# One attention group in steps of two items, with the copy of values in 17 parts and a later norm and split in the filling

## The chip, the cores and the metric

The kernel runs on one core of a Trainium2 chip. Its time is the device time of one execution in microseconds; given are the median of the runs shown and, from one profiled execution, where the time went. The core has five engines with a queue each, which run side by side and wait for one another by semaphores: PE (matrix products and transposes), DVE and ACT (element work on rows, both can read PE's result banks), POOL (element work in on-chip memory) and SP (here: it starts transfers). ACT starts some transfers too. Each engine takes its instructions strictly in the order in which they were queued.

## The reference, cut to what matters

One layer of a bidirectional encoder on 2048 tokens of 1024 numbers, in float32:

```
u   = rmsnorm(x, g_pre_mix)
qa, ka, va, qb, kb, vb = split(u @ w_in)
o_a = rmsnorm(windowed_gqa_sink(qa, ka, va, table, sink_a), g_out_a)
o_b = rmsnorm(dilated_mixture(qb, kb, vb, table), g_out_b)
h   = x + rmsnorm(concat(o_a, o_b) @ w_o, g_post_mix)
h   = h + rmsnorm(relu(rmsnorm(h, g_pre_mlp) @ w_up)**2 @ w_down, g_post_mlp)
h   = h + rmsnorm(sigmoid(h @ w_g + b_g) * (p @ w_p), g_post_ple)
```

Group a (`windowed_gqa_sink`) has 8 heads of 64 numbers. A block of 128 queries sees the key block before it, its own and the next; the logits get a bias by relative position, and a sink logit per head joins maximum and denominator. Group b (`dilated_mixture`) has 8 heads and three patterns (dilation 1, 4, 16), whose outputs are mixed by a softmax over their log-denominators.

## The kernel before

Every float32 product of the projections and of the feed-forward part is made of three: each factor is split into a high part (rounded to the fast float32 format) and the low rest, and high x high, high x low and low x high are summed. In the attention, products are plain float32.

The stages in order: projection of the first tokens and of the values; group a; group b; output projection with the first norms; feed-forward part; gate and output. From group a on, the order on each engine is the order in which the program writes the instructions (`manual_schedule`).

*Group a.* An item is a pair of heads and a block of 128 queries; there are 4 x 16 = 64 items, numbered 0 to 63. `a_item` gives an item four stages:
- `scores` (L502): two products on PE, one for each head of the pair, into two of the three banks of `ps_s`. For the blocks in the middle a row has 384 keys, for the first and last block of a pair 256.
- `probs`: first `normalise` for the item before (L479 on DVE: reciprocal of the denominators; L481 on POOL: two scalings). Then a small copy on POOL (L509, the sink logit), and for each head on DVE bias and row minimum in one (L513) and on ACT the exponential with its row sum (L517). L513 is what frees a bank of scores.
- `turn` (L526): PE transposes the probabilities into the two banks of `ps_t`, DVE (L531) and ACT (L529) copy them out.
- `values` (L542): the products with the values into the one bank of `ps_o`; ACT copies four items out (L547).

`Pipe` runs them shifted against each other. At step t it issues the scores of item t, the values of item t-3, the transposes of item t-2, the probabilities of item t, and then calls `feed(t)`. `later(dt, fn)` files work under a later step, and `tick()` at the end of a step issues what is due.

*The pieces in group a.* `feed` takes one piece of a generator, `rest_of_qk`, that makes the projections of group b's q and k for the second half of the tokens: 8 chunks of weights, for each two halves of tokens, for each of these one sum over 8 parts in a bank of `psm`. `mm3_pieces` yields after each two parts, so a piece is six products of 512 columns (L173 to L175) and there are 64. After the last piece of a sum the generator goes on at the next call: ACT copies the bank out (L229, L231) and starts the store. Between pieces the next chunk's weights are loaded, scaled and split, two parts in a step: the high half on ACT (L132), the low half on DVE directly behind it (L133). Five pieces run ahead of the loop.

Transfers also lie in the loop: `prefetch_a` loads the next pair's q in halves and its bias, and POOL reorders them two steps later (L235, L458). Ahead of the loop `relay_v` copies group b's values in DRAM to another layout, in three transfers (L375, L377).

*Group b.* Items of 2 x 2 blocks, three patterns and 4 pairs of heads: 96 items. Pattern 16 sees one key block (128 columns), the others two (256). PE order in a step: scores (L752), values (L796), transposes (L779), then `feed_b`. This takes a piece of `wo_first` in three of four steps: the first half of the output projection, for group a's result, tile by tile of 128 tokens. A tile has four calls: norm and first piece; second piece and evacuation (L898); first piece of the second half, then the split of the next tile; second piece and evacuation. `norm` (L612) is a product with a column of ones into a bank of `ps_t`, followed by one operation on DVE and one on POOL. The split (`halves`) takes ACT (L128 high, L605 squares), DVE (L129 low) and POOL (L606, L607). The lines of `wo_first` that matter:

```
ro = norm()
...
if hf == 0 and n == 0:
    halves, norm = load_o(wop, raws, "wraw", ps_t, "pt", oad, t + 1)
if hf == 1 and n == 0:
    nxt = halves()
```

Of the kernel before, what the change touches and what calls it, by code (L numbers as in the profile page):

```python
# [59 lines left out]
def layer(ctx, tc, a, out):  # L60
# [43 lines left out]
    gains = {}  # L104
# [7 lines left out]
    def row_ap(v, off, ap):  # L112
        return bass.AP(tensor=v.tensor, offset=v.offset + off, ap=ap)
# [54 lines left out]

    load_gain("pre_mix", a["g_pre_mix"])

    def mm3_pieces(ps, n, lh, ll, rh, rl, per=2):
        for k in range(n):
            pe.matmul(ps, lh(k), rh(k), start=k == 0, stop=False)  # L173
            pe.matmul(ps, lh(k), rl(k), start=False, stop=False)  # L174
            pe.matmul(ps, ll(k), rh(k), start=False, stop=k == n - 1)  # L175
            if k % per == per - 1:
                yield

    def run(gen):
# [33 lines left out]
    def proj_chunk(w, c, tb, psm, pst, tag):  # L213
        uh, ul = u[tb]
        ps = psm.tile([128, 512], F32, name="psm", tag="psm")
        yield from mm3_pieces(ps, 8, lambda k: w[:, 0, k], lambda k: w[:, 1, k], lambda k: uh[:, k], lambda k: ul[:, k])
        t = sg.tile([128, 512], F32, name="sgt", tag="sgt")
        if c == VA0:
            evac(t, ps)
            pt = pst.tile([128, 4, 128], F32, name=tag, tag=tag)  # L220
            for j in range(4):
                pe.transpose(pt[:, j, :], t[:, 128 * j : 128 * j + 128], ident)
            t = sg.tile([128, 512], F32, name="sgt", tag="sgt")
            evac(t, pt.rearrange("p j n -> p (j n)"))
            act.dma_start(vad[512 * tb : 512 * tb + 512, :].rearrange("(j a) n -> a j n", j=4),
                         t.rearrange("a (j n) -> a j n", j=4))
            return
        if c < 512 or 768 <= c < 1280:
            act.activation(t, ps, AF.Copy, scale=-0.125)  # L229
        else:  # L230
            act.activation(t, ps, AF.Copy)  # L231
        act.dma_start(qkd[chunk_of[c]][:, 512 * tb : 512 * tb + 512], t)
# [112 lines left out]


    att_ps = ExitStack()
    psm = att_ps.enter_context(tc.tile_pool(name="psm", bufs=2, space=PSUM, reuse_waits="tile"))
    ps_o = att_ps.enter_context(tc.tile_pool(name="ps_o", bufs=1, space=PSUM, reuse_waits="tile"))
    ps_t = att_ps.enter_context(tc.tile_pool(name="ps_t", bufs=2, space=PSUM, reuse_waits="tile"))  # L350
    ps_s = att_ps.enter_context(tc.tile_pool(name="ps_s", bufs=3, space=PSUM, reuse_waits="tile"))
    ordered = att_ps.enter_context(ExitStack())
    ordered.enter_context(tc.manual_schedule(engines=set(ORDERED)))

    HH = [slice(0, 64), slice(64, 128)]
    attb = ExitStack()
# [15 lines left out]

    def relay_v():
        n = 8 * VROW
        sp.dma_start(row_ap(vb1o, 0, [[n, 16], [VCHUNK, 15], [1, n]]), row_ap(vb3, 4 * VROW, [[VCHUNK, 16], [n, 15], [1, n]]))  # L375
        for i, a0 in ((0, 0), (2, 112)):
            sp.dma_start(row_ap(vb1a, i * VCHUNK, [[n, 16], [VCHUNK, 2], [1, n]]),  # L377
                         row_ap(vb3, a0 * VROW, [[VCHUNK, 16], [n, 2], [1, n]]))

    def load_v(pair, p):  # L380
        c0 = 128 * pair
# [39 lines left out]
    class Pipe:  # L421
# [18 lines left out]
        def drain(self):  # L440
            for _ in range(3):
                self.step()

    st_b = {}
    with ExitStack() as st:
        ap2 = st.enter_context(tc.tile_pool(name="ap2", bufs=1, reuse_waits="tile"))
# [27 lines left out]
                later(2 * i, lambda start=start: later(2, start()))  # L474

        def normalise():
            e, dn, off = st_a["rd"].pop(0)
            rd = sml.tile([128, 2], F32, name="rd", tag="rd")
            dve.reciprocal(rd, dn)  # L479
            for hh in range(2):  # L480
                pool.tensor_scalar(e[:, hh, off:384], e[:, hh, off:384], rd[:, hh : hh + 1], 1.0,  # L481
                                   op0=ALU.mult, op1=ALU.mult)

        def a_item(pair, n):
# [18 lines left out]
                              kk.rearrange("p r (k a) -> p k r a", a=8), start=True, stop=True)  # L503

            def probs():
                if st_a["rd"]:
                    normalise()
                e = box["e"] = ep.tile([128, 2, 392], F32, name="e", tag="e")
                pool.tensor_copy(e[:, :, 384], nsink[:, 2 * pair : 2 * pair + 2])  # L509
                dn = sml.tile([128, 2], F32, name="dn", tag="dn")  # L510
                for hh in range(2):
                    tm = sml.tile([128, 1], F32, name="tm", tag="tm")
                    dve.tensor_tensor_reduce(  # L513
                        e[:, hh, off:384], box["ps"][hh][:, 0:w], box["b"][hh][:, boff : boff + w], scale=1.0,
                        scalar=nsink[:, 2 * pair + hh : 2 * pair + hh + 1], op0=ALU.add, op1=ALU.min, accum_out=tm,
                    )
                    act.activation(e[:, hh, off:385], e[:, hh, off:385], AF.Exp, bias=tm, scale=-1.0,  # L517
                                   accum_out=dn[:, hh : hh + 1])
                st_a["rd"].append((e, dn, off))
# [29 lines left out]
                if n == 15:  # L549
                    act.dma_start(oad[128 * pair : 128 * pair + 128], st_a["o"])  # L550

            return scores, probs, turn, values

        def rest_of_qk():
            cs = [c for p in range(4) for c in (768 + 128 * p, 1280 + 128 * p)]
            w = w_next
            for i, c in enumerate(cs):
                nxt = raw = None
                for n, tb in enumerate((2, 3)):
                    for m, _ in enumerate(proj_chunk(w, c, tb, psm, ps_t, "pt")):  # L560
                        if i < 7 and n == 0 and m == 0:
                            raw = load_raw(cs[i + 1])
                            nxt = wcp.tile([128, 2, 8, 128], F32R, name="wc", tag="wc")
                        if i < 7 and 4 * n + m >= 3:
                            j = 4 * n + m - 3
                            split_chunk(nxt, raw, range(2 * j, min(2 * j + 2, 8)))
                        yield
                w = nxt

        fill = rest_of_qk()  # L570
        for _ in range(5):
            next(fill)
        for kb in range(16):
            sp.dma_start(va[:, kb, :], row_ap(vad, 8 * kb * 128, [[128 * 128, 16], [128, 8], [1, 128]]))
        relay_v()

        def feed(t):
            if t == 57:
                st_b["q"] = load_q(0)
                st_b["k"] = {0: load_k(0)}  # L580
# [3 lines left out]
                st_b["text"] = [load_text(1, hh) for hh in range(2)]  # L584
            next(fill, None)

        pipe = Pipe(feed)
        pipe.push([a_item(pair, n) for pair in range(4) for n in range(16)])
        normalise()
        pipe.drain()  # L590
        run(fill)
    att_a.close()
    u23.close()

# [58 lines left out]
    with ExitStack() as st:  # L653
# [222 lines left out]
        def wo_first():  # L876
# [4 lines left out]
            oh_, ol_ = halves()  # L881
            yield
            for t in range(16):
                ro = norm()
                for hf in range(2):
                    cs = slice(512 * hf, 512 * hf + 512)
                    ps = psm.tile([128, 512], F32, name="psm", tag="psm")
                    for n, _ in enumerate(mm3_pieces(ps, 4, lambda k: oh_[:, k, :], lambda k: ol_[:, k, :],
                                                     lambda k: wa[k][0][:, cs], lambda k: wa[k][1][:, cs])):
                        if t < 15:  # L890
                            if hf == 0 and n == 0:
                                halves, norm = load_o(wop, raws, "wraw", ps_t, "pt", oad, t + 1)
                            if hf == 1 and n == 0:
                                nxt = halves()
                        if n == 0:
                            yield
                    mx = sg.tile([128, 512], F32, name="sgt", tag="sgt")
                    act.activation(mx, ps, AF.Copy, scale=ro)  # L898
                    act.dma_start(mad[128 * t : 128 * t + 128, cs], mx)
                    yield  # L900
                if t < 15:
                    oh_, ol_ = nxt

        def ple():
            pw = [pl.tile([128, S], F32R, name="pw", tag=tag).rearrange("p (k n) -> p k n", k=2)
# [703 lines left out]
```

## Time and profile before

| | |
|---|---|
| median of 3 runs | 2789.16 us (2787.52 to 2789.19) |
| profiled execution | 2785.3 us, its span 2783.5 us |
| PE busy | 2709.7 us (97%) |
| weight loads of PE | 2126.0 us (76%) |
| DVE busy | 1755.0 us (63%) |
| ACT busy | 1272.0 us (46%) |
| POOL busy | 932.5 us (33%) |

Matmuls overlap, and their ends are modelled: a matmul that is slow to be followed by the next still counts as busy until its modelled end, so short waits of PE show better in the starts of its instructions than in its busy time. The idle time of an engine that nothing waits for costs nothing.

### The profile page before, as it was taken

The page shows a single profiled execution, that of the slowest core. Times are in us where ns is not written, and L with a number is a line of the kernel's source. Part 1 is how long each engine was busy: PE and PEld are TensorE (multiplying, and loading weights), DVE is VectorE, ACT ScalarE, POOL GpSimd, SP SyncE. Part 2 cuts the span into 40 slices and gives each one's busy share as a digit, 9 for nine tenths or more (in the row PEclk, how much of TensorE's full clock was granted, in tenths as well). Part 3 has the DMA queues.
Part 4 walks back from the last instruction along what each step waited for, and adds up shares of the span by engine and source line. Part 5 has one row for each costly group of instructions (what it writes and reads, how often), then busy time and mean ns, then how long its engine had stood idle before and what let it go on. Part 6 is the DMA issues. An engine that isn't in the chain of part 4 may idle for free.

```text
span 2783.5 us, 38953 instructions
## 1 busy us (share of the span) xinstructions
PE 2709.7 (97%) x13952; PEld 2126.0 (76%) x13952; DVE 1755.0 (63%) x3423; ACT 1272.0 (46%) x2947; POOL 932.5 (33%) x950
## 2 busy tenths in 40 slices
PE   7999999998999999999999999999999999999998
PEld 6878866666676777787888888888888888887877
DVE  4210234446666563677777777777777778887675
ACT  4321345556555564556444444344544344443422
POOL 3000033341323211435344354354354354353230
PEclk9999999999999999999999999999999999999999
DMA  6232252315424324873222222225323223334463
GB/s 179 78 122 80 99 159 75 113 62 156 130 70 129 90 96 150 274 258 101 90 65 76 69 65 74 78 100 203 115 75 106 81 79 99 108 100 172 169 212 106
DMA packets 247874, 324.39 MB, mean 117 GB/s; under 512 B 19905, under 2 KB 175553, under 8 KB 245281
## 3 DMA queue, kind: packets, MB, share of 16 engines
q1 hardware_dynamic: 220544, 281.73, 32.1%
q10 hardware_dynamic: 27136, 40.18, 4.0%
q8 instruction: 110, 1.80, 0.3%
q14 instruction: 84, 0.68, 0.1%
HBM read 227.16 MB, written 102.04 MB: 118 GB/s over the span
## 4 chain that ended last, share of the span: by engine, by line
PE 53%; DVE 1%; DMA 0%; issue 0%; ACT 0%; POOL 0%; DVEq 0%; POOLq 0%; SPq 0%; ACTq 0%
PE psd L1294 13%; PE psy L1294 10%; PE psu L175 9%; PE psu L173 8%; PE psu L174 8%; PE psm L139 2%; PE psm L138 2%; PE psm L137 2%; PE pst L146 0%; DVE dnl L1133 0%; DMA h<-hd 0%; DVE y L1565 0%; DMA upraw<-in_w_up_dram 0%; DVE al L1133 0%; DVE upl L1157 0%
## 5 line engine op out<-in xcount | busy, mean ns | idle before, releaser
L1303 DVE TENSOR_TENSOR acc<-acc,psd 128x512 f32<-128x512 f32 x488 | 332.3, 685 | 189.2 <-PE psd L1294 183.6
L175 PE MATMUL psu<-vt,upl 128*128 128x512 f32 x1024 | 406.8, 397 | 0.0
L173 PE MATMUL psu<-vt,uph 128*128 128x512 f32 x1024 | 404.7, 395 | 0.0
L174 PE MATMUL psu<-vt,uph 128*128 128x512 f32 x1024 | 400.5, 391 | 0.0
L1138 POOL TENSOR_TENSOR tmp<-rl 128x512 f32<-128x512 f32 x64 | 84.2, 1315 | 668.9 <-ACT rl L1282 668.9
L768 ACT ACTIVATE e<-e,tm 128x256 f32<-128x256 f32 (+1 forms) x384 | 176.7, 461 | 119.7 <-DVE tm L765 118.1
L173 PEld LDWEIGHTS psu<-vt,uph 128*128 128x128 f32 x1024 | 192.2, 188 | 46.8
L174 PEld LDWEIGHTS psu<-vt,uph 128*128 128x128 f32 x1024 | 192.3, 188 | 45.6
L175 PEld LDWEIGHTS psu<-vt,upl 128*128 128x128 f32 x1024 | 192.2, 188 | 45.7
L1303 DVE TENSOR_TENSOR acc<-acc,psy 128x512 f32<-128x512 f32 x248 | 170.1, 686 | 84.2 <-PE psy L1294 74.0
L1281 ACT ACTIVATE rl<-psu 128x512 f32<-128x512 f32 x128 | 76.4, 597 | 303.5 <-PE psu L175 303.3
L1301 POOL TENSOR_TENSOR acc<-acc,dmp 128x512 f32<-128x512 f32 x128 | 191.3, 1506 | 58.3 <-DVE al L1133 31.6
L133 DVE SCALAR_TENSOR_TENSOR wc<-wraw,pre_mix_t,wc 128x128 fp32r<-128x128 f32 x176 | 58.6, 380 | 232.8 <-ACT wc L132 232.8
L1294 PE MATMUL psd<-dnl,ah 128*128 128x512 f32 x512 | 203.4, 397 | 0.0
L1294 PE MATMUL psd<-dnh,al 128*128 128x512 f32 x512 | 202.5, 395 | 0.0
L1294 PE MATMUL psd<-dnh,ah 128*128 128x512 f32 x512 | 202.1, 395 | 0.0
L765 DVE CUSTOM_DVE_ANT_0 e<-ps_s,b 128x256 f32<-128x256 f32 (+1 forms) x384 | 122.6, 375 | 104.2 <-PE ps_s L752 104.0
L173 PE MATMUL psm<-uhi,wc 128*128 128x512 f32 x448 | 181.5, 410 | 0.3 <-ACT uhi L128 0.3
L175 PE MATMUL psm<-uhi,wc 128*128 128x512 f32 x448 | 178.0, 397 | 0.0
L174 PE MATMUL psm<-ulo,wc 128*128 128x512 f32 x448 | 177.8, 397 | 0.0
L1294 PE MATMUL psy<-dnh,ah 128*128 128x512 f32 x384 | 151.7, 395 | 3.1 <-ACT dmp L1300 2.9
L1294 PE MATMUL psy<-dnl,ah 128*128 128x512 f32 x384 | 152.6, 397 | 0.0
(699 smaller groups left out, 6246.3 us busy)
## 6 DMA issues: line engine op xcount, KB each, us to landing
upraw<-in_w_up_dram SPq DMA_DIRECT2D x64, 512.0 KB, 4.7
dnraw<-in_w_down_dram SPq DMA_DIRECT2D x64, 512.0 KB, 5.0
h<-hd SPq DMA_DIRECT2D x35, 512.0 KB, 7.1
xt<-in_x_dram SPq DMA_DIRECT2D x32, 512.0 KB, 4.1
wraw<-in_w_in_dram SPq DMA_DIRECT2D x26, 512.0 KB, 4.2
qkd<-sgt ACTq DMA_DIRECT2D x52, 256.0 KB, 2.5
mad<-sgt ACTq DMA_DIRECT2D x32, 256.0 KB, 2.0
acc<-mad SPq DMA_DIRECT2D x16, 512.0 KB, 6.6
```

The source lines that it names most:

```text
L133: dve.scalar_tensor_tensor(lo, src, g, hi.bitcast(F32), op0=ALU.mult, op1=ALU.subtract)
L137: pe.matmul(ps, lh(k), rh(k), start=k == 0, stop=False)
L173: pe.matmul(ps, lh(k), rh(k), start=k == 0, stop=False)
L174: pe.matmul(ps, lh(k), rl(k), start=False, stop=False)
L175: pe.matmul(ps, ll(k), rh(k), start=False, stop=k == n - 1)
L765: dve.tensor_tensor_reduce(ej, box["ps"][hh][:, 256 * jj : 256 * jj + w], bs[hh] if p == 2 else bs[hh][:, var], scale=1.0, scalar=3.0e38, ...
L768: act.activation(ej, ej, AF.Exp, bias=tm, scale=-1.0, accum_out=box["dn"][p][:, i : i + 1])
L1138: pool.tensor_tensor(t, x, y, op=op)
L1281: act.activation(rl, ps, AF.Relu)
L1294: pe.matmul(ps, l[:, js], r, start=start and m == 0, stop=m == 2, skip_group_check=True)
L1301: pool.tensor_tensor(t, t, d, op=ALU.add)
L1303: dve.tensor_add(t, t, ps)
```

## The change

- `Pipe2` takes the place of `Pipe` for group a. It issues two items in a step: the scores of items t and t+1, the normalisation of item t-1, the values of items t-4 and t-3, and then for each of the two: transposes (items t-2 and t-1), probabilities (items t and t+1), a call of `feed`, a tick.
- `normalise` becomes a stage of its own besides its call in `probs`; it returns at once where nothing is due.
- The banks in group a are dealt out anew: `ps_s` has 4 instead of 3, `psm` 1 instead of 2. Group b keeps its former numbers and gets its banks after group a.
- The last piece of a sum yields after its evacuation instead of before it. Six pieces instead of five run ahead of the loop.
- The low half of a weight part is filed one item later than its high half.
- `relay_v` becomes a generator of 17 transfers; `feed` takes one at every second item from item 16 on.
- In `wo_first` the norm is issued behind the first piece of a tile instead of ahead of it, and the split of the next tile behind the second half's evacuation instead of between its pieces.

```diff
-    def mm3_pieces(ps, n, lh, ll, rh, rl, per=2):
+    def mm3_pieces(ps, n, lh, ll, rh, rl, per=2, last=True):
...
-            if k % per == per - 1:
+            if k % per == per - 1 and (last or k < n - 1):
                 yield
...
+    def banks(st, n_m, n_s):
+        return [st.enter_context(tc.tile_pool(name=name, bufs=n, space=PSUM, reuse_waits="tile"))
+                for name, n in (("psm", n_m), ("ps_o", 1), ("ps_t", 2), ("ps_s", n_s))]
+
+    ps_a = ExitStack()
+    psm, ps_o, ps_t, ps_s = banks(ps_a, 1, 4)
...
     def relay_v():
         n = 8 * VROW
-        sp.dma_start(row_ap(vb1o, 0, [[n, 16], [VCHUNK, 15], [1, n]]), row_ap(vb3, 4 * VROW, [[VCHUNK, 16], [n, 15], [1, n]]))
         for i, a0 in ((0, 0), (2, 112)):
             sp.dma_start(row_ap(vb1a, i * VCHUNK, [[n, 16], [VCHUNK, 2], [1, n]]),
                          row_ap(vb3, a0 * VROW, [[VCHUNK, 16], [n, 2], [1, n]]))
+            yield
+        for c in range(15):
+            sp.dma_start(row_ap(vb1o, c * VCHUNK, [[n, 16], [1, n]]),
+                         row_ap(vb3, (4 + 8 * c) * VROW, [[VCHUNK, 16], [1, n]]))
+            yield
...
+    class Pipe2:
...
+        def do(self, stage_, n):
+            if 0 <= n < len(self.items):
+                self.items[n][stage_]()
+
+        def step(self):
+            t = self.t
+            self.do(0, t)
+            self.do(0, t + 1)
+            self.do(4, t - 1)
+            self.do(3, t - 4)
+            self.do(3, t - 3)
+            for n in range(2):
+                self.do(2, t - 2 + n)
+                self.do(1, t + n)
+                self.between(t + n)
+                tick()
+            self.t += 2
...
-            return scores, probs, turn, values
+            return scores, probs, turn, values, normalise
+
+        def split_part(w, raw, k):
+            g = gains["pre_mix"][:, k : k + 1]
+            act.activation(w[:, 0, k], raw[:, k], AF.Copy, scale=g)
+            later(1, lambda: dve.scalar_tensor_tensor(w[:, 1, k], raw[:, k], g, w[:, 0, k].bitcast(F32), op0=ALU.mult,
+                                                      op1=ALU.subtract))
...
-                    for m, _ in enumerate(proj_chunk(w, c, tb, psm, ps_t, "pt")):
+                    for m, _ in enumerate(itertools.chain(proj_chunk(w, c, tb, psm, ps_t, "pt"), [0])):
...
-                            split_chunk(nxt, raw, range(2 * j, min(2 * j + 2, 8)))
+                            for k in range(2 * j, min(2 * j + 2, 8)):
+                                split_part(nxt, raw, k)
...
-        for _ in range(5):
+        for _ in range(6):
             next(fill)
+            tick()
...
-        relay_v()
+        relay = relay_v()
 
         def feed(t):
+            if t % 2 == 0 and t > 14:
+                next(relay, None)
...
-        pipe = Pipe(feed)
+        pipe = Pipe2(feed)
         pipe.push([a_item(pair, n) for pair in range(4) for n in range(16)])
-        normalise()
         pipe.drain()
         run(fill)
+        run(relay)
+    ps_a.close()
+    psm, ps_o, ps_t, ps_s = banks(att_ps, 2, 3)
...
             for t in range(16):
-                ro = norm()
                 for hf in range(2):
...
-                        if t < 15:
-                            if hf == 0 and n == 0:
+                        if hf == 0 and n == 0:
+                            ro = norm()
+                            if t < 15:
                                 halves, norm = load_o(wop, raws, "wraw", ps_t, "pt", oad, t + 1)
-                            if hf == 1 and n == 0:
-                                nxt = halves()
                         if n == 0:
                             yield
...
+                    if hf == 1 and t < 15:
+                        oh_, ol_ = halves()
                     yield
-                if t < 15:
-                    oh_, ol_ = nxt
```

## Rows read from the trace of the kernel before

**Rows 1.** Groups of group a: instructions, shapes, count | busy us, mean ns | idle before, releaser.
```profile
L502 PEld LDWEIGHTS ps_s<-kt,q 64*128 64x128 f32 x256 | 26.1, 184 | 35.1 <-DVE tm L513 14.8 <-issue 14.4 <-DVE rd L479 4.0
L133 DVE SCALAR_TENSOR_TENSOR wc<-wraw,pre_mix_t,wc 128x128 fp32r<-128x128 f32 x54 | 17.5, 354 | 58.8 <-ACT wc L132 58.8
L517 ACT ACTIVATE e<-e,tm 128x385 f32<-128x385 f32 x112 | 68.2, 610 | 76.8 <-POOL e L509 76.8
L481 POOL TENSOR_SCALAR e<-e,rd 128x384 f32<-128x384 f32 x112 | 64.1, 585 | 133.9 <-DVE rd L479 133.8
L513 DVE CUSTOM_DVE_ANT_0 e<-ps_s,bt,nsink 128x384 f32<-128x384 f32 x112 | 63.6, 606 | 0.0
L531 DVE COPY et<-pt 128x384 f32<-128x384 f32 x56 | 31.1, 555 | 74.4 <-PE pt L526 74.4
```

**Rows 2.** PE timeline, start and duration in us: a whole item; a narrow one's values, transposes.
```profile
480.07 0.92 PE L502 MATMUL ps_s<-kt,q 64*128 64x384 f32 x4
480.91 0.88 PE L542 MATMUL po<-et,va 128*64 128x128 f32 x12
481.72 0.87 PE L526 MATMUL pt<-ident,e 128*128 128x128 f32 x6
482.35 0.48 PE L173 MATMUL psm<-uhi,wc 128*128 128x512 f32 x1
...
483.92 0.70 PE L502 MATMUL ps_s<-kt,q 64*128 64x256 f32 x4
...
432.23 0.66 PE L542 MATMUL po<-et,va 128*64 128x128 f32 x8
432.81 0.66 PE L526 MATMUL pt<-ident,e 128*128 128x128 f32 x4
```

**Rows 3.** PE timeline: scores of items 0, 59, 60 and 61, and of group b.
```profile
361.25 0.70 PE L502 MATMUL ps_s<-kt,q 64*128 64x256 f32 x4
...
596.01 0.92 PE L502 MATMUL ps_s<-kt,q 64*128 64x384 f32 x4
...
598.47 0.91 PE L502 MATMUL ps_s<-kt,q 64*128 64x384 f32 x2
...
601.91 0.91 PE L502 MATMUL ps_s<-kt,q 64*128 64x384 f32 x2
...
618.22 0.93 PE L752 MATMUL ps_s<-bk,bq 64*128 64x128 f32 x10
```

**Rows 4.** Groups of group b's stretch: the norm, and one tile's split.
```profile
L612 PE MATMUL pss<-ones,o 128*128 128x1 f32 x32 | 5.9, 255 | 6.8 <-DVE et L782 6.8
L129 DVE TENSOR_TENSOR ol__6759<-o,oh__6758 128x512 fp32r<-128x512 f32 x1 | 0.7, 692 | 5.3 <-ACT oh__6758 L128 5.3
L128 ACT ACTIVATE oh__6758<-o 128x512 fp32r<-128x512 f32 x1 | 0.6, 629 | 3.8 <-DMA o<-oad 3.8
```

**Rows 5.** Timeline of group b: transposes and what follows; an evacuation; late scores.
```profile
690.25 1.09 PE L779 MATMUL pt<-ident,e 128*128 128x128 f32 x8
691.10 0.48 PE L173 MATMUL psm<-wo,oh__5994 128*128 128x512 f32 x1
...
692.77 0.69 ACT L898 ACTIVATE sgt<-psm,ro 128x512 f32<-128x512 f32 x1 [0.42 <-PE psm L175]
...
694.94 1.09 PE L779 MATMUL pt<-ident,e 128*128 128x128 f32 x8
...
696.47 0.35 PE L612 MATMUL pss<-ones,o 128*128 128x1 f32 x2 [0.44 <-DVE et L782]
...
736.37 1.00 PE L752 MATMUL ps_s<-bk,bq 64*128 64x128 f32 x5 [3.21 <-DVE tm L765]
```

**Rows 6.** Windows: PE, PEld, DVE, ACT, POOL busy us; granted clock; DMA share, GB/s.
```profile
602.00:608.00 6.00, 5.84 (x39) 3.02 (x39) 3.07 (x12) 3.20 (x10) 2.55 (x6) 1.00 0.12 44
735.00:750.00 15.00, 12.59 (x62) 8.94 (x62) 8.77 (x37) 7.60 (x29) 4.73 (x7) 0.66 0.53 185
960.00:975.00 15.00, 13.45 (x54) 9.37 (x53) 7.37 (x28) 6.52 (x27) 4.68 (x7) 0.54 0.09 33
```

More of the change, by code (lines that the diff above doesn't have):

```diff
@@ L215, in proj_chunk @@
         ps = psm.tile([128, 512], F32, name="psm", tag="psm")
-        yield from mm3_pieces(ps, 8, lambda k: w[:, 0, k], lambda k: w[:, 1, k], lambda k: uh[:, k], lambda k: ul[:, k])
+        yield from mm3_pieces(ps, 8, lambda k: w[:, 0, k], lambda k: w[:, 1, k], lambda k: uh[:, k], lambda k: ul[:, k],
+                              last=False)
         t = sg.tile([128, 512], F32, name="sgt", tag="sgt")
@@ L347, in layer @@
     att_ps = ExitStack()
[L348 to L353, printed above, removed]
+    att_ps.enter_context(tc.manual_schedule(engines=set(ORDERED)))
+    def banks(st, n_m, n_s):
[3 more added lines that the diff above has]
+    psm, ps_o, ps_t, ps_s = banks(ps_a, 1, 4)
     HH = [slice(0, 64), slice(64, 128)]
@@ L442, in drain, with __init__, push @@
                 self.step()
+    class Pipe2:
+        def __init__(self, between):
+            self.items, self.t, self.between = [], 0, between
+        def do(self, stage_, n):
[14 more added lines that the diff above has]
+            self.t += 2
+        def push(self, items):
+            for item in items:
+                self.items.append(item)
+                if len(self.items) % 2 == 0:
+                    self.step()
+        def drain(self):
+            for _ in range(2):
+                self.step()
     st_b = {}
@@ L476, in normalise @@
         def normalise():
+            if not st_a["rd"]:
+                return
             e, dn, off = st_a["rd"].pop(0)
@@ L505, in probs @@
             def probs():
-                if st_a["rd"]:
-                    normalise()
+                normalise()
                 e = box["e"] = ep.tile([128, 2, 392], F32, name="e", tag="e")
@@ L585, in feed @@
             next(fill, None)
-        pipe = Pipe(feed)
+        pipe = Pipe2(feed)
         pipe.push([a_item(pair, n) for pair in range(4) for n in range(16)])
-        normalise()
         pipe.drain()
         run(fill)
+        run(relay)
+    ps_a.close()
+    psm, ps_o, ps_t, ps_s = banks(att_ps, 2, 3)
     att_a.close()
```

## The prediction

> **What bounds the kernel now.** I read the page first: PE is busy 97% of the span, and the chain that ended last is PE almost throughout, so the time is PE's own work plus what PE loses where the view of busy time cannot show it. The change touches group a's loop, the filling pieces in it, the copy of values and one generator in group b, so I went on with the groups of group a's stretch [rows 1], the PE timeline of single items [rows 2, 3], the groups and the timeline of group b [rows 4, 5], and the clock [rows 6].
>
> The weight loads of the score matmuls wait 14.8 us for `DVE tm L513`, the row minima that free the score banks, and DVE itself stands 58.8 us waiting for `ACT wc L132` [rows 1]: the low half of each weight part is queued on DVE directly behind its high half, and that one stands on ACT behind two exponentials. Whatever DVE has next (copy of transposes, reciprocal, minima) is late by that wait, and then the next scores are.
>
> How much it costs comes from item lengths. An undisturbed item with three key blocks takes 483.92 - 480.07 = 3.85 us of PE: scores 0.84, values 0.81, transposes 0.63, piece 1.57 [rows 2]. The 59 items with a piece run from 361.25 to 596.01 = 234.8 us [rows 3]. Their own work: 59 x 3.85 = 227.2, less 7 items at an edge with two key blocks (a third less of 2.28, about 0.7 each, 4.9), less the values and transposes that the first items do not have yet (3 x 0.81 + 2 x 0.63 = 3.7): 218.6. So 16.2 us are stalls, though PE looks busy in them.
>
> **The change part by part, against the profiled execution.**
>
> *Group a in steps of two.* PE's order becomes S S V V T F T F (scores, values, transposes, piece). The number of pieces stays 64.
> - Stalls. The low half is now queued one item later, so its high half is long done when DVE reaches it, and the 58.8 us of waiting go. What is late next: with four score banks the second S of a step needs the minima of the item just before, the last of the previous step. Worked through with 0 at the step's start and the durations of [rows 1]: the transposes feeding that item's slot begin at -2.2 (0.63 and 1.57 before), DVE's copy can start 0.4 later and ends at -1.2, reciprocal and both minima (0.6 each) end at +0.1; the second S begins at +0.84. Slack 0.7 us. The second T of the step needs the normalisation of its item: minima +0.1, two exponentials (0.61 each, behind POOL's small copy) +1.9, two scalings on POOL (0.59 each) +3.2; PE reaches that T after S S V V T F, 1.7 + 1.5 + 0.6 + 1.6 = +5.4. Slack 2.2 us. POOL's long reorder copies of the next q now fall behind the first item of a step, in POOL's hole between +3.4 and +6.3. So 16.2 us of stalls should go; I keep 2 for first steps and late loads. Bounds: 0 kept, or 10 kept (two fifths of the items still late by 0.4).
> - Joined values. A V of 12 records takes 0.81, one of 8 takes 432.81 - 432.23 = 0.58 [rows 2]; 4 records cost 0.23, so 0.12 of each V is switching. 27 joined pairs save 3.2 us (bounds 0 and 5).
> - One bank for the pieces (`psm`). Chunks end in the second half of a step, and PE's next piece comes after S S V V T, 3.8 us later. ACT's evacuation stands behind two exponentials and ends about 2.6 us into the step: hidden by 1.2 us. Without that cover each of 15 chunk ends would cost what is uncovered. Only in the six pieces ahead of the loop is there no cover: about 0.9 us, once.
> - The end. One item more runs without a piece (six, not five). Such items take 601.91 - 598.47 = 3.44 us now against 2.28 of PE work [rows 3]: the chain transposes, copy, minima, exponential, scaling sets them. In pairs the same links give about 6.5 us for a step, 3.25 an item, plus a drain of the same links. I count 0, bounds -4.6 (no chain left) and +3.
>
> *Values copied in 17 parts.* The copy that goes out as three transfers ahead of the loop goes out as 17 from item 16 on, each with its own issue on SP between the loads of weights and q. All end near item 48, ahead of group b's first use. Cost 0, hidden by the 7.6 us between a load of q and its use; if a part delays a q half past that, POOL waits in its hole first.
>
> Group a: -16.2 + 2 - 3.2 + 0.9 = **-16.5 us** (-23 to -4).
>
> *Group b's filling, norm.* The norm's small matmul takes one of the two transpose banks and therefore waits for DVE's copy of the transposes just made: T begins 694.94, norm 696.47, 1.53 us, where T to a piece takes 691.10 - 690.25 = 0.85 [rows 5]. So 0.68 us is lost per norm; the idle time put down to it is 6.8 us in all [rows 4], the floor; 16 x 0.68 = 10.9 is the ceiling. Behind the piece (1.57 us) the bank is free. I take -8.
>
> *Group b's filling, split.* The split comes one call later, behind the last evacuation.
> - In two places it waits for its input: 3.8 us on ACT for the high half, and DVE behind that 5.3 us [rows 4]; PE's scores then sit idle 3.21 us [rows 5]; afterwards the granted clock is 0.66 over 15 us, and 0.54 after the other place [rows 6]: 5.1 and 6.9 us of clock. A call later the input is there or nearly. Idle time: up to 5 us, I take -2.6. Clock: 0 to -12, I take -4, since part of that stretch waits for the mixer and not for PE.
> - Against it: evacuation 0.69 (it starts at 692.77 [rows 5]), the issue of its store about 0.3, high half 0.63, subtraction 0.69 [rows 4]: the low half is ready 2.3 us after the evacuation starts. In a wide step PE would begin the next piece at 694.94 + 0.85 = 695.79, 3.0 us after: hidden. In the narrow steps of pattern 16 S, V and T are about 1 us shorter, so some 5 tiles miss 0.3: +1.5. DVE's minima of the next item start 1.2 us late behind the subtraction; its next deadline is a step later. Upper bound 16 x 1.2 = 19.
>
> Group b: -8 - 2.6 - 4 + 1.5 = **-13 us** (-25 to +8).
>
> Sum: -29.5 on the profiled execution's 2785.3 us gives 2755.8. The median of the runs shown is 2789.2, 3.9 above it, so I predict **2760 us** for a median.
>
> **The rivals.**
> - *Half of group a's stalls stay.* If exponentials, high halves, evacuation and its store add up on ACT, the reciprocal comes late and with it the second S: slack is only 0.7 us. 8 us remain: 2768. For it: a step with split and evacuation gives ACT four exponentials, four high halves, two copies and an evacuation, and some of them lie between one exponential and the next. Against it: DVE no longer waits on high halves.
> - *Group b gives the norm alone.* The inputs of the split land later too, since their load is issued one piece later. Then neither the idle time nor the clock comes back, and the norm gives its floor: 2760 + 6.6 + 1.2 = 2768.
> - *More than I count.* All stalls, the end's chain and most of the clock: 2747.
> - *Slower: group b's subtraction lies on the path.* In each of 16 tiles PE waits for the low half, DVE's minima queue behind it, ACT's exponentials behind the squares. At the full 2.3 us a tile 37 us are lost against -24.5 (group a and the norm): 2802. It decides from 24.5 / 16 = 1.5 us a tile. For it: ACT and DVE are queued in order, and the wait now begins only when PE's piece ends. Against it: the 3.0 us of cover.
> [...]
>
> **How the numbers follow.** Forecast 0.50 (2752 to 2766), group a's stalls 0.15, norm alone 0.18, more 0.08, subtraction 0.06, clock 0.03. A measurement of this kernel tells 0.2% from no change, 5.6 us. The first four are faster, 0.91; both shortfalls together with the uncovered evacuations would come to about nothing, 0.05, of which I take 0.04 from these and 0.01 from the subtraction's weak end: faster 0.87, same 0.05, slower 0.08. Range 2745 to 2781: from the better case to both shortfalls at their bounds.
>
> **What would show it.** Right: DVE's wait for `ACT wc` near 0; 29 steps of about 7.6 us; group b's first scores near 602; no idle time at the norm; the split's copy without a DMA wait and the clock near 1.00 at the second and fourth pair's start. Wrong: score loads still waiting for `DVE tm`; pieces waiting for `ACT sgt`; pieces in group b waiting for `DVE ol`; a granted clock under 1.00 in group a.

## The result, and the profile after

The changed kernel takes 2750.6 us (median; 2747.0 to 2752.4) where the kernel before, run beside it, takes 2788.3 us (2783.8 to 2789.2): ratio 0.9862, 95% interval 0.985 to 0.9874, so 37.7 us less. The profiled executions stand at spans of 2783.5 and 2750.0 us, 33.5 apart: the profiled execution of before was one of its quicker ones, and that matters below.

Three windows, cut at the first scores of group a, the first scores of group b and one and the same item of group b near its end, place the gain. Columns as in [rows 6]. Before:

```profile
361.20:618.20 257.00, 251.47 (x1715) 164.67 (x1714) 120.27 (x438) 142.52 (x404) 98.22 (x205) 1.00 0.30 95
618.20:1042.70 424.50, 395.90 (x3099) 298.11 (x3098) 276.99 (x1058) 257.07 (x900) 106.47 (x150) 0.96 0.42 115
1042.70:2783.50 1740.80, 1716.54 (x7617) 1386.01 (x7616) 1280.45 (x1738) 765.36 (x1395) 692.46 (x553) 1.00 0.36 121
```

After:

```profile
363.70:588.60 224.90, 220.53 (x1709) 163.20 (x1708) 122.88 (x436) 139.95 (x400) 98.68 (x204) 1.00 0.32 107
588.60:1008.80 420.20, 394.37 (x3100) 297.37 (x3098) 276.67 (x1057) 256.31 (x898) 103.17 (x149) 0.97 0.43 116
1008.80:2750.00 1741.20, 1716.35 (x7617) 1388.02 (x7616) 1282.15 (x1739) 765.92 (x1397) 694.26 (x555) 1.00 0.36 121
```

Group a is 32.1 us shorter; 2.5 us are given back by its later start (one piece more ahead of it, 1.57, and 0.9 of waiting), so 29.6 us remain. Group b gives 4.3 in these two executions. The rest of the kernel is the same. The granted clock is 1.00 over all of group a in both.

The PE timeline of one step of two items in group a (start, duration; the other products of the pieces left out):

```profile
436.79 1.56 PE L545 MATMUL ps_s<-kt,q 64*128 64x384 f32 x8
438.28 1.53 PE L584 MATMUL po<-et,va 128*64 128x128 f32 x24
439.74 0.87 PE L568 MATMUL pt<-ident,e 128*128 128x128 f32 x6
440.37 0.48 PE L173 MATMUL psm<-uhi,wc 128*128 128x512 f32 x1
...
441.85 0.82 PE L568 MATMUL pt<-ident,e 128*128 128x128 f32 x6
442.42 0.48 PE L173 MATMUL psm<-uhi,wc 128*128 128x512 f32 x1
...
443.98 1.56 PE L545 MATMUL ps_s<-kt,q 64*128 64x384 f32 x8
```

From start to start: scores 1.49, values 1.46, transposes 0.63, piece 1.48, transposes 0.57, piece 1.56; a step is 7.19 us. Every step of two middle blocks is like this; two undisturbed items took 7.70 before [rows 2]. The groups of the same stretch (columns as in [rows 1]):

```profile
L545 PEld LDWEIGHTS ps_s<-kt,q 64*128 64x128 f32 x256 | 22.9, 186 | 21.1 <-issue 8.7 <-DVE tm L555 5.2 <-DVE wc L599 0.4
L584 PEld LDWEIGHTS po<-et,va 128*64 128x64 f32 x736 | 39.7, 137 | 16.4 <-issue 15.8 <-ACT et L571 0.6
L599 DVE SCALAR_TENSOR_TENSOR wc<-wraw,pre_mix_t,wc 128x128 fp32r<-128x128 f32 x52 | 17.3, 372 | 0.0
```

DVE no longer waits for the high half: 58.8 us [rows 1] have become 0.0. The loads of the scores wait 5.2 us for the minima instead of 14.8, and PE itself only in the two last steps, which hold no piece. And the loads' idle time put down to "issue" is down from 14.4 [rows 1] to 8.7.

In group b the norm no longer waits for DVE's copy (6.8 us before [rows 4]; 2.6 us of idle time are left ahead of it, of them 2.4 put down to `POOL o L661`). But in the narrow steps of pattern 16 something else is late. PE, then ACT, in one of them (idle time ahead of an instruction and its releaser in brackets):

```profile
687.14 0.66 PE L833 MATMUL pt<-ident,e 128*128 128x128 f32 x4
688.50 0.50 PE L173 MATMUL psm<-wo,oh__6596 128*128 128x512 f32 x1 [0.70 <-ACT oh__6596 L128]
...
691.24 0.38 PE L666 MATMUL pss<-ones,o 128*128 128x1 f32 x2 [0.82 <-POOL o L661]
```

```profile
686.72 0.69 ACT L950 ACTIVATE sgt<-psm,ro 128x512 f32<-128x512 f32 x1 [1.30 <-PE ps_s L806]
687.43 0.34 ACTq L951 DMA_DIRECT2D mad<-sgt  x1
687.82 0.63 ACT L128 ACTIVATE oh__6596<-o 128x512 fp32r<-128x512 f32 x1 [0.42 <-ACT sgt L950]
```

ACT evacuates, issues the store and makes the high half only then. Four transposes take 0.41 us where the piece behind them is in time (694.66 to 695.07), so PE wants the piece at 687.55; it starts at 688.50. Then the norm waits 0.82 us for POOL's sums of squares, which come behind the split: from the piece to the norm 2.74 us pass, not 1.57.

In two steps with wide products it is DVE that is late. Its subtraction waits for ACT's high half, as in group a before; the minima and the copy of transposes queue behind it, and the values wait (DVE, then PE, in the first of them):

```profile
787.83 0.69 DVE L129 TENSOR_TENSOR ol__7659<-o,oh__7658 128x512 fp32r<-128x512 f32 x1 [2.29 <-ACT oh__7658 L128]
790.55 0.43 PE L850 MATMUL po<-et,v 128*64 128x128 f32 x2 [0.57 <-DVE et L836]
```

The clock where the second and the fourth pair start, after; the first window stands for the second of [rows 6], the other is 35 us long:

```profile
705.00:720.00 15.00, 13.12 (x68) 9.03 (x66) 7.20 (x28) 6.88 (x23) 4.59 (x7) 0.77 0.69 222
920.00:955.00 35.00, 31.55 (x188) 21.96 (x188) 23.57 (x92) 18.67 (x67) 11.03 (x17) 0.90 0.49 103
```

and the 35 us before:

```profile
945.00:980.00 35.00, 30.62 (x187) 21.89 (x187) 21.21 (x89) 16.96 (x65) 6.87 (x12) 0.80 0.48 96
```

The granted clock is higher at both places, 0.77 against 0.66 and 0.90 against 0.80 (15 x 0.11 = 1.7 us and 35 x 0.10 = 3.5 us, as an estimate), but it is not at 1.00.

### The profile page after: what moved, and what is told of

It reads as the page before. It is cut to its first block, busy times and chain, and to the rows that moved or that the text cites. A ratio compares the mean times of both kernels' runs of the same rounds, so it can differ in the third digit from the quotient of the medians.

```text
span 2750.0 us, 38984 instructions
## 1 busy us (share of the span) xinstructions
PE 2679.0 (97%) x13952; PEld 2127.2 (77%) x13952; DVE 1759.4 (64%) x3423; ACT 1270.6 (46%) x2947; POOL 931.2 (34%) x950
## 4 chain that ended last, share of the span: by engine, by line
PE 52%; DVE 2%; ACT 1%; DMA 1%; issue 1%; POOL 0%; DVEq 0%; POOLq 0%; SPq 0%; ACTq 0%
PE psd L1346 13%; PE psy L1346 10%; PE psu L175 9%; PE psu L173 8%; PE psu L174 8%; PE psm L139 1%; PE psm L138 1%; PE psm L137 1%; DVE y L1617 0%; PE pst L146 0%; DVE dnl L1185 0%; DVE al L1185 0%; DMA out_dram<-y 0%; ACT dmp L1394 0%; DVE y L1600 0%
## 5 line engine op out<-in xcount | busy, mean ns | idle before, releaser
L173 PE MATMUL psu<-vt,uph 128*128 128x512 f32 x1024 | 404.9, 395 | 0.0
L174 PE MATMUL psu<-vt,uph 128*128 128x512 f32 x1024 | 400.8, 391 | 0.0
L173 PEld LDWEIGHTS psu<-vt,uph 128*128 128x128 f32 x1024 | 192.5, 188 | 46.3
L174 PEld LDWEIGHTS psu<-vt,uph 128*128 128x128 f32 x1024 | 192.4, 188 | 45.2
L173 PE MATMUL psm<-uhi,wc 128*128 128x512 f32 x448 | 181.6, 410 | 1.0 <-ACT sgt L230 0.7
L174 PE MATMUL psm<-ulo,wc 128*128 128x512 f32 x448 | 178.1, 397 | 0.0
L1346 PE MATMUL psy<-dnh,al 128*128 128x512 f32 x384 | 151.7, 395 | 0.0
```

The source lines that it names most:

```text
L1346: pe.matmul(ps, l[:, js], r, start=start and m == 0, stop=m == 2, skip_group_check=True)
```

## The experiments

Ratios are against the kernel before, run beside each experiment on the same chip, with 95% intervals. The experiments ran on three other chips than the changed kernel; there the median of the kernel before was 2789.1, 2789.5 and 2787.2 us, so the difference of two medians from different chips is good to some 2 us at best. "Length of group a" is from its first scores to those of group b in the profiled execution: 257.0 us before, 224.9 after.

**Group a alone.** The changed kernel with the `wo_first` of before.

> The changed kernel with group b's filling generator as it was before (norm ahead of the piece, split between the pieces). Theory: the two parts do not touch each other, and the trace after gives -29.6 us up to group b's first scores and -4.3 from there on. So 2788.3 - 37.7 + 4.3, about 2755, with group b's first scores at 588.6 again and 0.6 us lost at each norm in a wide step again. Rival: group b's part is worth the -13 of the prediction and group a's less than the trace shows, because group b starts in another state of its loads: then 2763 or more. A second rival: group b's part costs more than it gives, then under 2749.

2759.2 us, 0.9898 (0.9883 to 0.9913): 30 us less than before; length of group a 224.9. What group b's change adds on top is 8.6 us of medians. The profile gives group b, whose code is here that of before, 9 us more than there:

```profile
588.40:1022.00 433.60, 403.57 (x3100) 301.97 (x3098) 277.96 (x1058) 257.20 (x900) 105.97 (x151) 0.94 0.42 113
```

The same code of group b thus varies by several us between executions, and the granted clock accounts for it. Length times mean granted clock is an estimate of the length at the full clock (good to some 2 us, as the clock is given to 0.01): 424.5 x 0.96 = 407.5 before, 433.6 x 0.94 = 407.6 here. The changed kernel's group b comes to 420.2 x 0.97 = 407.6. So at equal clock group b's change as a whole gains about nothing, and by the same estimate the 8.6 us between the medians are mostly clock: over all runs the mean clock of the whole kernel is 0.9896 here and 0.9925 in the changed kernel, and 2755 x 0.0029 is 8.0 us. That the change itself raised the clock is not shown.

**The low half later, by itself.** The kernel before, with one edit:

```
-split_chunk(nxt, raw, ...)          # low half behind high half
+act.activation(w[:, 0, k], ...)
+later(1, lambda: dve.scalar_tensor_tensor(w[:, 1, k], ...))
```

> The kernel before with one thing changed: in group a's weight parts the low half is queued on DVE one item after the high half. Items are not joined, banks and everything else stay. Theory: the 16.2 us of stalls in group a come from DVE standing behind ACT's high half; DVE's wait for the high half goes from 58.8 us to near 0 and the 59 items from 234.8 to about 219 us: 2788.3 - 16 = 2772. Rival: with three score banks and one item per step DVE's order has no slack anyway, so the scores stay late even without that wait; stalls stay at 8 to 16 us: 2780 to 2788.

2769.5 us, 0.9935 (0.9921 to 0.9948); length of group a 243.0, so 13.9 of the 16.2 us of stalls are gone. The theory holds. What is left shows among the waits of group a (total us, times, longest):

```profile
PEld ps_s L502 <- DVE tm L513: 4.9, 10, 0.7
ACT wc L556 <- DMA wraw<-in_w_in_dram: 3.6, 1, 3.6
DVE wc L557 <- ACT wc L556: 1.8, 1, 1.8
```

ACT stands once for 3.6 us before the weights of the next chunk, for their load: a stall that has nothing to do with DVE's order (see the copy of values below).

**The low half at once, in steps of two.** The changed kernel with that edit undone.

> The changed kernel with the low halves queued directly behind the high halves again, steps of two items kept. Theory (the stalls come from DVE behind the high half, whatever the order): DVE waits 30 to 60 us for ACT again, steps with weight parts are late by about 1 us, 13 to 16 us come back: 2764 to 2767. Rival: a step of 7.2 us with four score banks has slack enough (0.7 us at the second scores, 2.2 at the second transposes by the prediction) and the wait is swallowed: 2751 to 2754, and then the joined order by itself had removed the stalls.

2767.4 us, 0.9924 (0.991 to 0.9938); length 239.1, so 14.2 us come back, as the theory said. Waits of group a:

```profile
DVE wc L133 <- ACT wc L132: 48.7, 25, 3.0
PEld ps_s L545 <- DVE tm L555: 16.6, 26, 1.3
```

Joining items does not remove the stalls; moving the low half does, in either order of items.

**Scores and values apart.** The order in a step S V S V T F T F:

```
 self.do(0, t)
-self.do(0, t + 1)
 self.do(4, t - 1)
 self.do(3, t - 4)
+self.do(0, t + 1)
 self.do(3, t - 3)
```

> The changed kernel with the order S V S V T F T F in a step, where it is S S V V T F T F: the scores and the values of the two items are no longer joined, everything else stays. Theory: every boundary between kinds of small matmuls costs PE, 0.19 us for scores to values (two joined scores take 1.49, two single ones 2 x 0.84) and 0.16 for values (1.46 against 2 x 0.81): 29 steps x 0.35 = 10 us come back, step 7.55 us: 2761. Rival (the prediction's size): only the values' switching of 0.12 counts: 3 us, 2754. Second rival: the shorter steps come from the stalls that are gone alone, then no change: 2751.

2759.0 us, 0.9892 (0.9877 to 0.9908), 8.4 more than the changed kernel; length 233.4, 8.5 more. PE timeline of a step:

```profile
439.81 0.92 PE L545 MATMUL ps_s<-kt,q 64*128 64x384 f32 x4
440.65 0.88 PE L584 MATMUL po<-et,va 128*64 128x128 f32 x12
441.46 0.92 PE L545 MATMUL ps_s<-kt,q 64*128 64x384 f32 x4
...
447.36 0.92 PE L545 MATMUL ps_s<-kt,q 64*128 64x384 f32 x4
```

7.55 us, and scores and values are back at 0.84 and 0.81 (439.81 to 440.65 to 441.46). So these boundaries between kinds of products cost PE 0.36 us a step (7.55 against 7.19), and its timeline shows no wait for another engine in this step.

**The copy of values at once.** The changed kernel with the three transfers ahead of the loop.

```
-    next(relay, None)      # a part every other item from item 16 on
+relay_v()                  # three transfers ahead of the loop
```

> The changed kernel with the copy of values as it was, three transfers issued ahead of group a's loop, not 17 from item 16 on. Theory: the copy is off the path either way, 2751, within 2 us. Rival: the large transfers run beside the loads of group a's values and first queries and delay the first steps: 2753 to 2756.

2758.2 us, 0.9892 (0.9875 to 0.9909). Both miss: 7.6 us more than the changed kernel, above the rival's price too. Length of group a 230.8, 5.9 more, nearly all of it in one step that takes 12.41 us. ACT, then PE in it, and the window around the loads (DMA share and GB/s at the end), first of this kernel:

```profile
387.80 0.69 ACT L594 ACTIVATE wc<-wraw,pre_mix_t 128x128 fp32r<-128x128 f32 x2 [5.79 <-DMA wraw<-in_w_in_dram]
```

```profile
389.50 0.52 PE L564 MATMUL pt<-ident,e 128*128 128x128 f32 x3 [4.15 <-ACT et L567]
```

```profile
365.00:385.00 20.00, 20.00 (x139) 14.53 (x138) 10.71 (x39) 10.38 (x31) 7.45 (x18) 1.00 0.91 289
```

and the same window of the changed kernel:

```profile
365.00:385.00 20.00, 20.00 (x138) 14.63 (x137) 10.74 (x40) 12.57 (x36) 7.44 (x18) 1.00 0.30 98
```

In the kernel before it was:

```profile
365.00:385.00 20.00, 20.00 (x129) 12.89 (x129) 9.96 (x37) 10.43 (x29) 7.32 (x18) 1.00 0.93 286
```

With the copy at once the DMA engines are busy to 0.91 for 20 us, and a load of 512 KB of weights, issued behind it, lands late: ACT waits 5.79 us for it, with the copies of transposes and the exponentials behind it. In the changed kernel the same load, issued at 367.29, landed 4.5 us later; in the kernel before, issued at 368.03, it released ACT only at 387.20, but ACT had waited only 0.7 us for it, as its steps were late too.

**The norm later, the split as before.** The changed kernel with

```
+if hf == 1 and n == 0 and t < 15:
+    nxt = halves()
...
 if hf == 1 and t < 15:
-    oh_, ol_ = halves()
+    oh_, ol_ = nxt
```

> The changed kernel with group b's split back between the two pieces of a tile's second half, as it was; the norm stays behind the first piece. Theory, from the trace after held against that of group a's change alone: the norm gives 0.6 us in seven wide steps, 4.1 us, and nothing in the narrow ones; the split's move is a trade, it gives 5.1 + 5.6 + 3.3 us and some clock where the second and fourth pair start, and costs 1.2 to 3.5 us in each of six narrow or mixer steps (11.7 us in all). So this kernel is 4 us faster than group a alone (2759.2) and slower than the changed one: 2755. Pieces of 2.74 us in narrow steps gone, scores of 5 to 6 us at 700 to 715 and 930 to 945 back. Rival: the norm alone carries group b's gain, and the split's place is worth nothing on balance: 2751.

2744.4 us, 0.9837 (0.9823 to 0.985): 6.2 less than the changed kernel, and less than both expectations. My theory had read the norm's worth from the trace after, where the late split hides part of it. Here eleven norms give 0.7 to 0.8 us each against group a alone, 8.4 us. The medians differ by 14.8; the mean clock of the runs went from 0.9896 to 0.9920, which is 6.6 of them as an estimate, and 8.2 are left. The norms, first with group a alone, then here:

```profile
L666 PE MATMUL pss<-ones,o 128*128 128x1 f32 x30 | 5.9, 266 | 6.3 <-DVE et L836 6.3
```

```profile
L666 PE MATMUL pss<-ones,o 128*128 128x1 f32 x32 | 4.5, 210 | 0.2 <-DVE et L836 0.2
```

The narrow step shown above now runs without a wait, and the stall at the second pair's start is back:

```profile
685.84 0.66 PE L833 MATMUL pt<-ident,e 128*128 128x128 f32 x4
686.26 0.48 PE L173 MATMUL psm<-wo,oh__6523 128*128 128x512 f32 x1
...
687.73 0.28 PE L666 MATMUL pss<-ones,o 128*128 128x1 f32 x2
...
704.29 1.22 PE L806 MATMUL ps_s<-bk,bq 64*128 64x128 f32 x6 [3.58 <-DVE tm L819]
```

So the split's later place was a loss: it gave some 5 to 6 us at each of two pair starts and took more back in the steps between. At equal clock the loss is larger than the medians say, since group b here is

```profile
587.80:1001.90 414.10, 389.33 (x3100) 298.42 (x3098) 277.47 (x1058) 257.15 (x900) 107.03 (x151) 0.96 0.44 118
```

and 414.1 x 0.96 = 397.5, some 10 us under the changed kernel's 407.6.

**The split ahead of the evacuation.** As in the changed kernel, but `halves()` stands before the copy out and its store.

> The changed kernel with the split queued ahead of the tile's last evacuation and its store instead of behind them, same call. Theory: what is late in narrow steps is ACT's high half, behind the evacuation (0.66) and the issue of its store (0.34); one microsecond earlier it makes the pieces of 2.74 us start on time, 1.2 us in four or five steps, and part of the mixer's 2.3 and 3.5: 2743 to 2746. Rival: the squares now stand ahead of the evacuation and push it and the next exponentials by 1.3 us, so the minima and scores of the next step are late: 2751 or more. Second rival: the wait for the split's load comes back at the pair starts: 2755.

2745.8 us, 0.9843 (0.983 to 0.9856): within the theory's range, 4.8 less than the changed kernel. The order on ACT was a cause: group b comes to 416.1 x 0.96 = 399.5, so at equal clock most of the loss is gone. The medians show less of it, as steps at the pair starts ran at a lower clock (one takes 9.30 us at 0.51, in the changed kernel 5.83 at 1.00); that all of the loss is ACT's order is not shown.

**The norm later, on the kernel before.**

> The kernel before with one thing changed: in group b the norm's small matmul comes behind the tile's first piece. Group a and the split as before. Theory: eleven norms in wide steps give 0.77 us each, as the trace of the norm alone on top of group a's change shows them, 8.5 us: 2789 - 8.5 = 2781; what that pair of medians had beyond it (14.8 us) came from stretches of the lower clock that differ with the position of the transfers, not from the norm. Rival: the norm is worth 14.8 here too: 2774.5. Second rival: only the seven norms that the trace after shows at 0.6 us count: 2785.

2775.5 us, 0.9959 (0.9944 to 0.9974), that is 7 to 16 us less: theory (8.5) and first rival (14.8) both lie in it, the second rival (4) does not. The mean clock of all runs speaks for the theory: it is 0.9920 against 0.9911, as an estimate 2.5 of the 11.7 us between the medians, and 9.2 are left. The eleven steps of the trace give 8.4. That the position of the transfers sets the stretches of the lower clock is not shown.

**The split late at two tiles only.** As the norm alone, but `halves()` behind the evacuation where `t in (2, 11)`.

> The changed kernel with the norm behind the first piece and the split between the pieces again, except for the third and the twelfth tile, where it comes behind the evacuation. Those two stand where the second and fourth pair start, and their load is late. Theory: the narrow steps keep what the split between the pieces gave (2744.4 against 2750.6), and the two stalls of 5.4 and 6.3 us in that kernel's scores become some 2 to 3 us: 2738 to 2741. Rival: at those two places the late split costs in its own step what the stall cost, as the mixer stands there too: 2744.

2740.5 us, 0.9831 (0.9813 to 0.9848). That lies in the theory's range, but against the norm alone (0.9837) the intervals overlap, so the time decides nothing. Aligned item by item, this trace gains 5.1 us at the second pair's first scores and loses 5.2 in the four steps behind them, as the rival says, but not by its mechanism. The four steps here, and the same four, with the same code, in the last kernel below:

```profile
701.09:730.60 29.51, 28.53 (x145) 19.48 (x145) 18.02 (x59) 12.30 (x44) 11.81 (x18) 0.77 0.45 143
```

```profile
695.71:719.21 23.50, 22.34 (x145) 15.72 (x144) 17.55 (x59) 12.29 (x44) 11.80 (x18) 1.00 0.59 199
```

29.51 x 0.77 is 22.7: what the second pair's start gained was lost to the lower clock, not to the late split's own work.

**Fewer pieces ahead of group a.** `for _ in range(6)` became `range(2)`, and then was left out.

> The changed kernel with two pieces of the filling ahead of group a's loop, not six; the four others fall into the steps that ran without pieces at its end. Theory: ahead of the loop PE does nothing else with those 6.3 us, and at the end two pieceless steps of 5.0 and 6.7 us, set by the chain transposes, copy, minima, exponential, scaling, become two of 7.2 us: -6.3 + 2.7 = -3.6, and the 0.9 us wait for the single bank goes too: 2746. Rival: the first steps wait for their bias and values, which are then needed 6 us earlier: no change, 2751.

> The changed kernel with no piece ahead of group a's loop. Theory as with two ahead, one step further: -9.4 ahead, and the three last steps with scores get pieces, 5.0 + 6.7 + 6.5 become 3 x 7.2 = +3.4; with the 0.9 it is -6.9: 2744. Rival: the first scores, now wanted near 354, wait for POOL's copies of the bias that end at 356, and the first values for their loads: one to three microseconds less, 2746.

2744.1 us (0.9838, 0.9825 to 0.9851) and 2742.5 us (0.9834, 0.982 to 0.9847). With none ahead, group b's first scores start at

```profile
581.68 0.49 PE L803 MATMUL ps_s<-bk,bq 64*128 64x128 f32 x4
```

where they were at 588.61: the 6.9 us of the theory, to the tenth. The medians give 6.5 and 8.1 us.

**Both.** Split late at two tiles, and no pieces ahead.

> The kernel with the split late at two tiles only, and in addition no piece of the filling ahead of group a's loop. Theory: the two gains lie in different stretches and add, 8.1 us less than the former: 2731 to 2733. Rival: group b then starts before its loads, as with group a's change alone, and gives some of it back in its first steps: 2735 to 2738.

2728.8 us, 0.9791 (0.9771 to 0.981): better than both kernels, some 20 us below the changed one by the ratios, and below the expectation. Group b, to the same item as above, takes

```profile
582.20:983.60 401.40, 384.76 (x3099) 293.64 (x3097) 277.01 (x1058) 257.01 (x900) 106.38 (x151) 0.98 0.45 122
```

with a clock of 0.98. With the same code of group b the kernel before this one took 411.5 us at 0.95. At the full clock the two are estimated at 393.4 and 390.9, so the 10 us between them are clock, which would explain why the gains seem to more than add. Why this execution met so few stretches of the lower clock is open.

## Why the prediction was right, and where its sum was not

The time fell by 37.7 us where 29.5 were forecast. The direction and the range hold, but the terms are off in both directions, and part of the fall is clock. Group a gave nearly twice what it was to give, and group b about nothing at equal clock; that the sum still lies in the range is in part luck.

- *Stalls of group a, -16.2 with 2 kept: right.* The low half on DVE was the cause in both orders of items (13.9 and 14.2 us), and the slacks of 0.7 and 2.2 us sufficed. The remaining 2.3 us go with the late load of weights (the next point but one); in the order of single items that was not tried by itself.
- *Joined values, -3.2: the mis-sized term.* A pair of items costs 7.19 instead of 7.70 us, 0.51 x 29 = 14.8 as an estimate. I priced one boundary, that of the values, and only by extrapolating 12 and 8 records. The scores have one too: two take 1.49 against 2 x 0.84, and two values 1.46 against 2 x 0.81. This part was tested, and 8.5 us came back when it was undone. The rest is read from the step alone: a piece ahead of transposes takes 1.48 where one ahead of scores takes 1.57, and transposes behind a piece take 0.57 where those behind values take 0.63. So not every boundary costs: the one from a piece to transposes, which takes the place of one from a piece to scores and one from values to transposes, costs none of this. The sign stood in [rows 1]: 14.4 us of idle time of the scores' loads "issue", which I left out of the argument because it names no engine. It is now 8.7, and 14.6 with scores and values apart.
- *Values copied in 17 parts, 0: wrong.* It is worth 5.9 us of group a's length once the other stalls are gone. The prediction looked at what the copy's parts might delay and not at what the whole copy did delay: with the DMA engines at 0.91 for 20 us in that run, a load of weights came late, and ACT waited 5.79 us for it.
- *One bank, +0.9, and the end, 0: right.* Group a starts 2.48 us later, 1.57 of it the sixth piece. Its end takes 24.8 us where 22.2 were taken, for one item more (2.28): +0.3. That it could have been shortened by 6.9 us with pieces I did not see. The fourth score bank was not tried by itself.
- *Norm, -8: right as a direct gain* (8.4 in eleven places, 8.2 and 9.2 in the medians net of the clock). The 14.8 of the medians on top of group a alone hold 6.6 of clock, whose amount also varies between executions of the same code, so it is not shown that the norm causes it.
- *Split, -2.6 - 4 + 1.5: the step that failed.* Its place costs 6.2 us in the medians and some 10 at equal clock, so that of group b's -13 about nothing is left at equal clock. The gains exist: the score stalls at the two pair starts are gone, and the lower clock there takes some 5 us less by the estimate above (1.7 + 3.5), near the -4 of the prediction. But "ready 2.3 us after the evacuation starts, PE begins 3.0 us after" was taken from a wide step, with 1 us off for the narrow ones. In the narrow step shown, which also holds the mixer's copies and their transfer issues, ACT starts the evacuation late, and PE wants the piece 0.83 us after that start (687.55 - 686.72), not 2.0. And the norm of the next tile waits for POOL's sums, which stand behind ACT's squares and these behind the split; the prediction named no such wait.
- *The rivals.* PE's scores wait for minima in no step with pieces, so half of the stalls did not stay. (That rival's time should have been 2766: the forecast keeps 2 of the 8 us already.) "The norm alone" had the wrong reason: the stalls of the split's input did go, but other waits took their place. The slower rival exists in part. Five steps of pattern 16 lose 1.1 to 3.5 us against the norm alone: three through the high half and POOL's sums, two in waits for DVE's minima and its part of the mixer (one of these at a clock of 0.76). Two steps with wide products lose 0.8 to 0.9, where DVE's minima and copies queue behind the subtraction as the rival said. But these are a few tiles instead of sixteen. The clock's 0.03 of the forecast rests on nothing that a run shows: with scores, values and transposes in a row the granted clock of the changed kernel is 1.00 over all of group a (363.70 to 588.60).

Group a's surplus, the wrong split and the clock cancelled in part: a sum inside its range is no proof of its terms.

## What to carry to other kernels

Here idle time of the weight loads put down to "issue" at a change of kind of product (14.4 us for the scores, 8.7 after) went with a cost that the starts in a timeline price (0.19 us a pair for scores, 0.16 for values): where you find such, group products of one kind, and multiply by the number of those boundaries whose starts show a cost. Before you cost a moved transfer at nothing, read what stood behind it, in the window's DMA share and in who waits for a load. And when an operation is moved behind another on a shared queue, work out its deadline in the shortest step, with everything else that queue holds in it, not in a typical one. And where the granted clock differs between two executions, compare length times clock before you put a difference down to the code.

## What the runs showed of the hardware

In the step shown, joining saves 0.19 us a pair on scores and 0.16 on values. There PEld stands idle until the scores' products are nearly done, and the first load of the values starts together with their first product (438.28). Behind a piece, where the boundary costs nothing, the first load of the transposes starts 0.24 us ahead of their first product (441.85). Start and duration:

```profile
436.78 0.95 PEld L545 LDWEIGHTS ps_s<-kt,q 64*128 64x128 f32 x8 [0.36 <-issue]
438.27 0.42 PEld L584 LDWEIGHTS po<-et,va 128*64 128x64 f32 x8 [0.54 <-issue]
...
441.15 0.39 PE L173 MATMUL psm<-uhi,wc 128*128 128x512 f32 x1
441.16 0.19 PEld L174 LDWEIGHTS psm<-ulo,wc 128*128 128x128 f32 x1
...
441.61 0.81 PEld L568 LDWEIGHTS pt<-ident,e 128*128 128x128 f32 x6
```

In a piece of the same step a load lies beside a product: that of L174 (441.16 to 441.35) beside the product of L173 (441.15 to 441.54). Why a load comes late at some boundaries, 0.54 us from the scores to the values, is open.

The same code of group b took 424.5 and 433.6 us in two executions, with granted clocks of 0.96 and 0.94, and 401.4 and 411.5 in two others, with 0.98 and 0.95. Length times clock is the same within 3 us in each pair; a difference of a few us in that stretch can be clock alone.
